# Rotation and scaling of queries and keys read by DVE straight from PSUM, in two transformer blocks on one core

## The chip, the cores and the metric

The kernel runs on one core of a Trainium2 chip, as one program in one launch. The core has TensorE (PE, matmuls into PSUM), VectorE (DVE), ScalarE (ACT), GpSimd (POOL) and a DMA queue issued from SyncE (SP). The metric is the device time in microseconds, the median of 3 runs of the whole program; the time before is 1341.64 us (1341.46 to 1342.78).

## The reference

Two transformer blocks over 512 positions and 1024 channels, float32. What touches the change is how each makes its queries and keys:

```
# block 1: 12 heads of 64, one dilated attention with three configurations
h = rms_norm(x, ln_pre_mix);  proj = h @ w_in
q, k = rope(q, pos), rope(k, pos)          # x1*cos - x2*sin, x2*cos + x1*sin
# block 2: 16 heads of 64 (differential, forgetting, chunked)
hn = rms_norm_2(h, ln_mix);  z = hn @ w_in
q1 = rms_norm_2(split_heads(q1, 4), g[0])  # the same for q2, k1, k2, qf, kf, qc, kc
```

After them come softmax, weighing of the values, an output projection, and a gated MLP (block 1) or a gated MLP with a short convolution and a last gate (block 2).

## The kernel before

Activations lie transposed, channels on the 128 partitions and the 512 positions along a row, in 8 tiles. Every float32 matrix product is done as three matmuls: each operand is split into a rounded high part and a rest (`wunit` for weights, lines 164 and 167; `split` for activations, lines 176 to 182), and high x high, high x low and low x high are added in PSUM (lines 186 to 188, and 372 to 374 for the projections).

PSUM has 8 banks, in four pools: 3 banks "d" for all that `psum()` asks for, 2 "s" for scores, 2 "t" for transposed probabilities and 1 "v" (`BANKS`, line 31). Tile frees a bank when the last instruction that reads it is done. Small work tiles of 128 x 512 come from rings, of which "z" has 6 slots.

A mixing stage is played from a list (`ORDER1`, `ORDER2`): P is a projection, T its transposes and head operands, V values, S scores, W weighing, U the pooled branch's input, O an early part of the output projection, D the first two projections of block 2 side by side, F the forget gate's rows, G the gate product of the end. Block 1 begins "P0 P2 P1 T0 V0 S00", block 2 "G0 G1 D VM P3 T1 T0 S00". Program order is a priority only: the order on each engine is made when the kernel is built, by a list schedule over a simulated timeline, and each engine then works through its own list in that order.

A projection (`chunk`, line 357) yields 256 columns, queries and keys of two heads. It runs in two halves of 2 x 128 positions; a half fills one bank of pool "d" with 48 matmuls, and then calls `out_of`. The normalisation is folded in afterwards: projections are made of the unnormalised activations, and the row statistic, a sum of squares over all 8 activation tiles, enters later as a factor per position.

In block 1, P0 is done with its contraction outermost, so that it can follow the arrival of the input, and both its halves end together. `rstd_cols` (lines 246 to 253) makes the statistic `rc` from the sum of squares by small matmuls (L249), Ln and Exp on ACT (L112) and three DVE steps (L234 to L236). Line 470 scales cosines and sines by it into `rot`. `out_of` (lines 482 to 495) copies the bank to z on ACT (L485); POOL makes the two products with the sine (L490, L491) into y; DVE multiplies by the cosine (L492) and adds the halves (L493, L494). `to_heads` (line 310) transposes z on TensorE (L316) into two banks of pool "d", from which ACT and DVE make high and low parts (L328 to L331), and DMAs copy rows across partitions (L418).

In block 2, `out_of` (lines 698 to 716) copies the bank to z (L700), squares it on ACT (L701), sums over each head on DVE (L703), multiplies by `r2`, made of `rc` (L665 to L667, L706), and gets the inverse root by Ln, Exp and three DVE steps (L710, L711, L713; L712 multiplies by `r1`, also made of `rc`). POOL then multiplies z by the result (L715). D uses `chunks_beside` (line 382): two projections share the contraction loop, and two banks are filled at a time. For these, `rc` comes from the second `rstd_cols` call, at the end of `post`, over the output of block 1.

Of the kernel before, what the change touches and what calls it, by code (L numbers as in the profile page):

```python
# [11 lines left out]
AF = mybir.ActivationFunctionType  # L12
ALU = mybir.AluOpType
AX = mybir.AxisListType

P = 128
# [45 lines left out]
class Builder:  # L62
# [386 lines left out]
    def mix1(self):  # L449
        nc = self.nc  # L450
        io = self.io
        x, h = [], []
        early = self.units("w_qk1", 0)
        for k in range(KD):
            x.extend(self.load_x((k,)))
            h.append(self.split(x[k], self.col("ln_pre_mix", k), tag="h"))
            if k in (0, 4):
                early(k // 4)
        self.rest()
        rope = self.slot("m", F32, (P, 4, 96))  # L460
        nc.sync.dma_start(rope, io["rope"])
        nc.sync.dma_start(self.ident, io["ident"])
        acc = self.slot("m")
        for k in range(KD):
            self.square_acc(acc, x[k], k == 0, after=self.last)
        R = self.slot("m")
        rc = self.rstd_cols(acc)
        rot = self.slot("m", F32, (P, 4, 96))
        for t in range(4):
            nc.vector.tensor_scalar(rot[:, t], rope[:, t], rc[:, 2 * t:2 * t + 1], None, ALU.mult)  # L470
        tab = self.slot("m")
        nc.sync.dma_start(tab, io["tab_mult"])

        zs = {}
        ops = {}
        ps = {}
        outs = {}

        def project(i):
            zs[i] = []  # L480

            def out_of(t1, ps):
                t0 = t1 - 1
                z, y = self.slot("z"), self.slot("z")
                nc.scalar.activation(z, ps, AF.Copy)  # L485
                zv, yv = [a.rearrange("p (t h d) -> p t h d", t=2, d=64) for a in (z, y)]
                cs = rot[:, t0:t0 + 2, 0:64].unsqueeze(2).to_broadcast([P, 2, 4, 64])
                sn = rot[:, t0:t0 + 2, 64:96].unsqueeze(2).to_broadcast([P, 2, 4, 32])
                a, b = slice(0, 32), slice(32, 64)
                nc.gpsimd.tensor_tensor(yv[:, :, :, a], zv[:, :, :, b], sn, ALU.mult)  # L490
                nc.gpsimd.tensor_tensor(yv[:, :, :, b], zv[:, :, :, a], sn, ALU.mult)  # L491
                nc.vector.tensor_tensor(zv, zv, cs, ALU.mult)  # L492
                nc.vector.tensor_tensor(zv[:, :, :, a], zv[:, :, :, a], yv[:, :, :, a], ALU.subtract)  # L493
                nc.vector.tensor_tensor(zv[:, :, :, b], zv[:, :, :, b], yv[:, :, :, b], ALU.add)  # L494
                zs[i].append(z)
            self.chunk("w_qk1", int(i), h, 256, out_of, i == "0", early)

        def heads(i):
            ops[i] = self.to_heads(zs[i], -0.125, None)

        oT = [None] * 8
        vts = []

        def values(g):
            vt = self.v_tiles()
            vts.append(vt)
            self.chunk("w_v1", int(g), h, 256, lambda t, ps: self.put_v2(vt, t, ps, rc))

        def score(i, e, wide=False):
            ps[i + e] = self.scores(ops[i][int(e)], tab, wide)  # L510

        def weigh(i, e, wide=False):
            i, e, p = int(i), int(e), ps[i + e]
            if e == 0:
                outs[i] = self.slot("o")
            j = (2 * i + e) % 4
            self.weigh(p, [vts[i // 2][t][:, j, :] for t in range(4)], outs[i], e == 1, wide)
            if e == 1:
                oT[2 + i] = self.split(outs[i], tag="o")

        us = []
        get = self.units("w_u1")

        def pool_in(i):
            if i == "0":
                self.rstd_rows(acc, R)
            u = self.psum()
            self.slab(u, "w_u1", int(i), h, units=get)
            t = self.slot("z")
            nc.vector.tensor_tensor(t, u, R, ALU.mult)  # L530
            us.append(t)

        self.play(ORDER1, P=project, T=heads, V=values, S=score, W=weigh, U=pool_in,
                  B=lambda: self.pool_branch(us, oT))
        return self.post(oT, DONE1, "w_out", "ln_post_mix", "ln_pre_ffn", True)
# [120 lines left out]
    def mix2(self, h, rc):  # L656
        nc = self.nc
# [31 lines left out]
        ps = {}  # L689
# [5 lines left out]
        def projected(i):  # L695
            out = zs[i] = []

            def out_of(t1, ps):
                z, sq = self.slot("z"), self.slot("z")
                nc.scalar.activation(z, ps, AF.Copy)  # L700
                nc.scalar.activation(sq, ps, AF.Square)  # L701
                st = self.small(8)
                nc.vector.tensor_reduce(st, sq.rearrange("p (h d) -> p h d", d=64), AX.X, ALU.add)  # L703
                four = lambda v: v[:, t1 - 1:t1 + 1].unsqueeze(2).to_broadcast([P, 2, 4])
                two = lambda v: v.rearrange("p (t h) -> p t h", h=4)
                nc.vector.tensor_tensor(two(st), two(st), four(r2), ALU.mult)  # L706
                y, w = self.small(8), self.small(8)
                self.act(y, st, AF.Ln, bias=self.eps, scale=1.0)
                self.act(y, y, AF.Exp, scale=-0.5)
                nc.vector.scalar_tensor_tensor(w, st, EPS, y, ALU.add, ALU.mult)  # L710
                nc.vector.scalar_tensor_tensor(w, w, -0.5, y, ALU.mult, ALU.mult)  # L711
                nc.vector.tensor_tensor(two(y), two(y), four(r1), ALU.mult)  # L712
                nc.vector.scalar_tensor_tensor(st, w, 1.5, y, ALU.add, ALU.mult)  # L713
                zv = z.rearrange("p (h d) -> p h d", d=64)
                nc.gpsimd.tensor_tensor(zv, zv, st.unsqueeze(2).to_broadcast([P, 8, 64]), ALU.mult)  # L715
                out.append(z)
            return out_of

# [100 lines left out]
        for m in range(KD):  # L819
            t = self.slot("v")  # L820
# [254 lines left out]
```

## Time and profile before

| | |
|---|---|
| median of 3 runs | 1341.64 us |
| the profiled execution's own time | 1343.58 us |
| its span, first to last instruction | 1341.5 us |
| PE busy | 1311.8 us (98%) |
| DVE busy | 851.3 us (63%) |
| ACT busy | 672.6 us (50%) |
| POOL busy | 153.8 us (11%) |
| mean granted TensorE clock | 0.994 |

The profile is one execution. Times of instructions count from the span's start. "L485" is line 485 of the kernel; a helper's line stands for all its callers, so L112 is every Ln, Exp and other special function. A row of waits or of the timeline says in brackets or after an arrow how long the engine had stood idle and which instruction ended that. [...]

Block 1's mixing takes about the first 200 us, its output projection and MLP run to about 615 us, block 2's mixing from there to about 890 us, and block 2's MLP and end the rest.

### The profile page before, as it was taken

Reading aid. Unit: us, or ns where it says so; the run is one execution under the profiler, and the core shown is the slowest. Engines: PE = TensorE matmul, PEld = TensorE weight load, DVE = VectorE, ACT = ScalarE, POOL = GpSimd, SP = SyncE. Lnnn points to the kernel's source line nnn. Section 1 sums busy time; section 2 is a strip of 40 time slices with the busy share of each in tenths; the row PEclk is TensorE's granted clock in tenths of the full one; section 3 lists DMA queues with packets and bytes.
Section 4 is the critical chain, followed back from the end, with each engine's and each line's share of the span. In section 5 each row is a group of like instructions: output and inputs, shape, how many; then the busy total and the mean of one; then the engine's idle time right before and its main releaser. Section 6 shows DMA issues by size and latency. Waiting matters only on the chain.

```text
span 1341.5 us, 20064 instructions
## 1 busy us (share of the span) xinstructions
PE 1311.8 (98%) x7450; PEld 1138.0 (85%) x7450; DVE 851.3 (63%) x1771; ACT 672.6 (50%) x1327; POOL 153.8 (11%) x190
## 2 busy tenths in 40 slices
PE   9799999999999999999999999899999999999998
PEld 9799988988888888888988999779888888888887
DVE  7777885864444432229588878766877777733354
ACT  6466755543333332237576777755554444522241
POOL 1232220000000000001222334430000000000000
PEclk9999999999999999999999999999999999999999
DMA  6322334233333333228244445333332332332221
GB/s 228 109 67 68 95 111 126 70 117 96 96 95 95 94 95 94 95 70 262 88 112 117 123 117 138 93 106 124 126 95 95 94 95 94 102 95 94 94 79 63
DMA packets 48801, 141.69 MB, mean 106 GB/s; under 512 B 6240, under 2 KB 7136, under 8 KB 48704
## 3 DMA queue, kind: packets, MB, share of 16 engines
q1 hardware_dynamic: 48704, 140.42, 34.0%
q8 instruction: 58, 0.95, 0.3%
q14 instruction: 39, 0.32, 0.1%
HBM read 122.38 MB, written 6.29 MB: 96 GB/s over the span
## 4 chain that ended last, share of the span: by engine, by line
PE 84%; DVE 8%; DMA 3%; ACT 2%; issue 2%; SPq 1%; POOL 0%; DVEq 0%; ACTq 0%; POOLq 0%
PE p L186 21%; PE p L187 21%; PE p L188 21%; PE p L372 4%; PE p L373 4%; PE p L374 4%; DVE wl L167 2%; PE p L283 2%; PE p L292 1%; PE p L291 1%; PE p L261 1%; DVE sp L265 1%; PE p L262 1%; DMA wr<-in_w_qk 1%; ACT sp L112 1%
## 5 line engine op out<-in xcount | busy, mean ns | idle before, releaser
L164 ACT ACTIVATE wh<-wr 128x512 fp32r<-128x512 f32 x417 | 259.2, 630 | 405.4 <-PE p L187 351.9
L167 DVE TENSOR_TENSOR wl<-wr,wh 128x512 fp32r<-128x512 f32 (+1 forms) x400 | 286.2, 723 | 238.5 <-ACT wh L164 227.1
L188 PE MATMUL p<-sh,wl 128*128 128x512 f32 (+1 forms) x858 | 320.4, 377 | 0.0
L187 PE MATMUL p<-sh,wh 128*128 128x512 f32 (+1 forms) x858 | 319.5, 376 | 0.1
L186 PE MATMUL p<-sh,wh 128*128 128x512 f32 (+1 forms) x858 | 311.0, 375 | 1.0 <-ACT sh L179 0.7
L372 PE MATMUL p<-wh,sh 128*128 128x256 f32 (+1 forms) x672 | 193.3, 289 | 5.8 <-ACT sz L485 3.3
L373 PE MATMUL p<-wl,sh 128*128 128x256 f32 (+1 forms) x672 | 192.1, 287 | 0.3 <-DVE wl L167 0.2
L374 PE MATMUL p<-wh,sh 128*128 128x256 f32 (+1 forms) x672 | 191.2, 286 | 0.0
L187 PEld LDWEIGHTS p<-sh,wh 128*128 128x128 f32 x858 | 161.2, 188 | 32.6 <-issue 0.5
L188 PEld LDWEIGHTS p<-sh,wl 128*128 128x128 f32 x858 | 161.2, 188 | 31.8 <-issue 0.7
L186 PEld LDWEIGHTS p<-sh,wh 128*128 128x128 f32 x858 | 157.2, 188 | 33.4 <-ACT sh L179 1.1
L372 PEld LDWEIGHTS p<-wh,sh 128*128 128x128 f32 x672 | 128.7, 192 | 9.1 <-ACT sz L485 3.6
L373 PEld LDWEIGHTS p<-wl,sh 128*128 128x128 f32 x672 | 128.9, 192 | 1.1 <-DVE wl L167 0.8
L374 PEld LDWEIGHTS p<-wh,sh 128*128 128x128 f32 x672 | 128.6, 192 | 1.1 <-issue 0.5
L273 POOL TENSOR_SCALAR sp<-sp,m 128x128 f32<-128x128 f32 (+1 forms) x112 | 72.0, 647 | 186.3 <-DVE m L269 145.5
L112 ACT ACTIVATE sp<-sp,m 128x128 f32<-128x128 f32 (+3 forms) x128 | 71.5, 560 | 36.4 <-DVE m L265 33.8
L188 PE MATMUL p<-so,wl 128*128 128x512 f32 (+1 forms) x246 | 88.5, 360 | 0.0
L187 PE MATMUL p<-so,wh 128*128 128x512 f32 (+1 forms) x246 | 88.5, 360 | 0.0
L186 PE MATMUL p<-so,wh 128*128 128x512 f32 (+1 forms) x246 | 87.6, 361 | 0.6 <-DVE m L265 0.5
L167 POOL TENSOR_TENSOR wl<-wr,wh 128x512 fp32r<-128x512 f32 (+1 forms) x17 | 23.8, 1402 | 455.3 <-ACT wh L164 443.7
L265 DVE CUSTOM_DVE_ANT_0 sp<-p,sm 128x128 f32<-128x128 f32 (+3 forms) x128 | 60.4, 483 | 17.3 <-PE p L262 13.5
L187 PE MATMUL p<-sk,wh 128*128 128x512 f32 (+1 forms) x184 | 67.1, 365 | 0.0
(205 smaller groups left out, 2138.8 us busy)
## 6 DMA issues: line engine op xcount, KB each, us to landing
wr<-in_w_gu SPq DMA_DIRECT2D x88, 512.0 KB
wr<-in_w_down SPq DMA_DIRECT2D x44, 512.0 KB
wr<-in_w_qk SPq DMA_DIRECT2D x31, 512.0 KB
sk<-sk SPq DMA_DIRECT2D x88, 128.0 KB
wr<-in_w_out SPq DMA_DIRECT2D x12, 512.0 KB
sv<-in_x SPq DMA_DIRECT2D x16, 256.0 KB
wr<-in_w_ple_gate SPq DMA_DIRECT2D x8, 512.0 KB
wr<-in_w_v SPq DMA_DIRECT2D x6, 512.0 KB
```

The lines of the kernel that those rows point to most:

```text
L112: i = self.nc.scalar.activation(out, in_, func, **k)
L164: nc.scalar.activation(hi[:, :w], c, AF.Copy)
L167: eng.tensor_tensor(lo[:, :w], c, hi[:, :w].bitcast(F32), ALU.subtract)
L186: mm(out, lhsT=ahi, rhs=bhi, start=start, stop=False)
L187: mm(out, lhsT=ahi, rhs=blo, start=False, stop=False)
L188: mm(out, lhsT=alo, rhs=bhi, start=False, stop=stop)
L265: nc.vector.tensor_tensor_reduce(p[:, :n], ps[:, :n], tab[:, (3 - qb) * P:S], 1.0, 3e38, ALU.add, ALU.min, accum_out=m[:, 0:1])
L273: self.nc.gpsimd.tensor_scalar(p[:, :n], p[:, :n], m[:, 2:3], 1.0, ALU.mult, ALU.mult)
L283: ins = nc.tensor.transpose(pt[:, w:w + P], ps_list[qb][:, kb * P:kb * P + P], self.ident)
L372: mm(d, lhsT=h[k][0][:, a], rhs=hi[:, c], start=k == 0 and (o == 0 or not first), stop=False)
L373: mm(d, lhsT=h[k][0][:, a], rhs=lo[:, c], start=False, stop=False)
L374: mm(d, lhsT=h[k][1][:, a], rhs=hi[:, c], start=False, stop=k == 7 and (o > 0 or not first))
```

## The change

In block 1 ACT's copy of the bank is gone. DVE makes the product with the cosine and both products with the sine straight from PSUM, and the two last steps are as before. In block 2 the copy is gone too, and the product with the inverse root is made by DVE from PSUM into z in place of POOL's from z to z. The square still reads the bank on ACT. Nothing else is edited.

```
--- before.py
+++ after.py
@@ -482,14 +482,13 @@
             def out_of(t1, ps):
                 t0 = t1 - 1
                 z, y = self.slot("z"), self.slot("z")
-                nc.scalar.activation(z, ps, AF.Copy)
-                zv, yv = [a.rearrange("p (t h d) -> p t h d", t=2, d=64) for a in (z, y)]
+                zv, yv, pv = [a.rearrange("p (t h d) -> p t h d", t=2, d=64) for a in (z, y, ps)]
                 cs = rot[:, t0:t0 + 2, 0:64].unsqueeze(2).to_broadcast([P, 2, 4, 64])
                 sn = rot[:, t0:t0 + 2, 64:96].unsqueeze(2).to_broadcast([P, 2, 4, 32])
                 a, b = slice(0, 32), slice(32, 64)
-                nc.gpsimd.tensor_tensor(yv[:, :, :, a], zv[:, :, :, b], sn, ALU.mult)
-                nc.gpsimd.tensor_tensor(yv[:, :, :, b], zv[:, :, :, a], sn, ALU.mult)
-                nc.vector.tensor_tensor(zv, zv, cs, ALU.mult)
+                nc.vector.tensor_tensor(zv, pv, cs, ALU.mult)
+                nc.vector.tensor_tensor(yv[:, :, :, a], pv[:, :, :, b], sn, ALU.mult)
+                nc.vector.tensor_tensor(yv[:, :, :, b], pv[:, :, :, a], sn, ALU.mult)
                 nc.vector.tensor_tensor(zv[:, :, :, a], zv[:, :, :, a], yv[:, :, :, a], ALU.subtract)
                 nc.vector.tensor_tensor(zv[:, :, :, b], zv[:, :, :, b], yv[:, :, :, b], ALU.add)
                 zs[i].append(z)
@@ -697,7 +696,6 @@
 
             def out_of(t1, ps):
                 z, sq = self.slot("z"), self.slot("z")
-                nc.scalar.activation(z, ps, AF.Copy)
                 nc.scalar.activation(sq, ps, AF.Square)
                 st = self.small(8)
                 nc.vector.tensor_reduce(st, sq.rearrange("p (h d) -> p h d", d=64), AX.X, ALU.add)
@@ -711,8 +709,8 @@
                 nc.vector.scalar_tensor_tensor(w, w, -0.5, y, ALU.mult, ALU.mult)
                 nc.vector.tensor_tensor(two(y), two(y), four(r1), ALU.mult)
                 nc.vector.scalar_tensor_tensor(st, w, 1.5, y, ALU.add, ALU.mult)
-                zv = z.rearrange("p (h d) -> p h d", d=64)
-                nc.gpsimd.tensor_tensor(zv, zv, st.unsqueeze(2).to_broadcast([P, 8, 64]), ALU.mult)
+                zv, pv = [a.rearrange("p (h d) -> p h d", d=64) for a in (z, ps)]
+                nc.vector.tensor_tensor(zv, pv, st.unsqueeze(2).to_broadcast([P, 8, 64]), ALU.mult)
                 out.append(z)
             return out_of
 
```

## Rows read from the trace of the kernel before

**Rows 1.** The page: busy time of each engine; the chain that ended last.
```profile
PE 1311.8 (98%) x7450; PEld 1138.0 (85%) x7450; DVE 851.3 (63%) x1771; ACT 672.6 (50%) x1327; POOL 153.8 (11%) x190
PE 84%; DVE 8%; DMA 3%; ACT 2%; issue 2%; SPq 1%; POOL 0%; DVEq 0%; ACTq 0%; POOLq 0%
```
**Rows 2.** TensorE's waits: waiter, releaser: total us, times, longest us.
```profile
PE p L372 <- ACT sz L485: 3.3, 1, 3.3
...
PE p L261 <- DMA sk<-sk: 2.3, 1, 2.3
```
**Rows 3.** Timeline, start of block 1: start us, duration us, engine, line.
```profile
17.99 0.57 ACT L485 ACTIVATE sz<-p 128x512 f32<-128x512 f32 x1
...
24.05 0.95 PE L249 MATMUL p<-ones,sm 128*128 128x2 f32 x8
...
27.59 0.97 DVE L470 TENSOR_SCALAR sm<-sm,rc 128x96 f32<-128x96 f32 x4
...
41.54 1.03 PE L316 MATMUL p<-ident,sz 128*128 128x128 f32 x8
```
**Rows 4.** Windows: stretch and length, busy us per engine, granted clock, DMA.
```profile
45.90:51.60 5.70, 5.68 (x48) 5.68 (x48) 5.61 (x9) 2.63 (x5) 2.16 (x2) 1.00 0.56 176
...
54.20:58.20 4.00, 4.00 (x21) 4.00 (x22) 0.14 (x1) 0.00 (x0) 0.00 (x0) 0.57 0.08 18
...
640.00:860.00 220.00, 210.83 (x1637) 200.29 (x1636) 175.90 (x520) 155.25 (x374) 75.08 (x88) 0.99 0.40 113
```
**Rows 5.** Groups by line: count, then busy us, mean ns, idle before.
```profile
L167 DVE TENSOR_TENSOR wl<-wr,wh 128x512 fp32r<-128x512 f32 (+1 forms) x400 | 286.2, 723 | 238.5 <-ACT wh L164 227.1 <-PE p L187 5.2 <-PE p L188 3.5
...
L898 DVE TENSOR_TENSOR sz<-p,sm 128x512 f32<-128x512 f32 x44 | 30.3, 688 | 27.1 <-PE p L188 27.0
...
L715 POOL TENSOR_TENSOR sz<-sz,m 128x512 f32<-128x512 f32 x20 | 22.5, 1124 | 41.9 <-DVE m L713 34.5 <-ACT st L295 4.4 <-DVE m L269 2.9
...
L908 DVE TENSOR_TENSOR sz<-sz,sz 128x512 f32<-128x512 f32 x22 | 15.1, 686 | 0.0
...
L700 ACT ACTIVATE sz<-p 128x512 f32<-128x512 f32 x20 | 11.9, 593 | 5.6 <-PE p L374 4.3 <-PE p L397 1.1
...
L490 POOL TENSOR_TENSOR sz<-sz,sm 128x256 f32<-128x256 f32 x12 | 11.3, 945 | 47.9 <-DVE sm L470 27.3 <-ACT sz L485 15.7 <-DVE sz L494 4.9
...
L492 DVE TENSOR_TENSOR sz<-sz,sm 128x512 f32<-128x512 f32 x12 | 8.7, 729 | 5.1 <-POOL sz L491 5.1
...
L485 ACT ACTIVATE sz<-p 128x512 f32<-128x512 f32 x12 | 7.0, 592 | 8.9 <-DVE sz L494 7.1 <-PE p L374 1.7
...
L493 DVE TENSOR_TENSOR sz<-sz,sz 128x256 f32<-128x256 f32 x12 | 5.7, 472 | 0.1
```
**Rows 6.** Timelines of ACT, PE and DVE at the start of block 2.
```profile
635.46 0.58 ACT L701 ACTIVATE sz<-p 128x512 f32<-128x512 f32 x1
...
637.93 0.41 PE L395 MATMUL p<-wh,sh 128*128 128x256 f32 x1
...
641.82 0.50 PE L249 MATMUL p<-ones,sz 128*128 128x2 f32 x4
...
643.64 0.17 DVE L236 SCALAR_TENSOR_TENSOR rc<-m,rc 128x8 f32<-128x8 f32 x1
...
648.72 0.17 DVE L713 SCALAR_TENSOR_TENSOR m<-m,m 128x8 f32<-128x8 f32 x1
```
**Rows 7.** Timelines of ACT, DVE and PE, 663 to 682 us.
```profile
663.24 0.60 ACT L700 ACTIVATE sz<-p 128x512 f32<-128x512 f32 x1 [1.82 <-PE p L374]
...
665.08 0.17 DVE L706 TENSOR_TENSOR m<-m,r 128x8 f32<-128x8 f32 x1
...
666.46 0.17 DVE L713 SCALAR_TENSOR_TENSOR m<-m,m 128x8 f32<-128x8 f32 x1
...
673.97 0.63 PE L316 MATMUL p<-ident,sz 128*128 128x128 f32 x4 [1.40 <-DVE sk L329]
...
681.34 0.34 PE L261 MATMUL p<-sk,sk 128*128 128x128 f32 x2
```

More of the change, by code (lines that the diff above doesn't have):

```diff
@@ L484, in out_of @@
                 z, y = self.slot("z"), self.slot("z")
-                nc.scalar.activation(z, ps, AF.Copy)
-                zv, yv = [a.rearrange("p (t h d) -> p t h d", t=2, d=64) for a in (z, y)]
+                zv, yv, pv = [a.rearrange("p (t h d) -> p t h d", t=2, d=64) for a in (z, y, ps)]
                 cs = rot[:, t0:t0 + 2, 0:64].unsqueeze(2).to_broadcast([P, 2, 4, 64])
@@ L489, in out_of @@
                 a, b = slice(0, 32), slice(32, 64)
-                nc.gpsimd.tensor_tensor(yv[:, :, :, a], zv[:, :, :, b], sn, ALU.mult)
-                nc.gpsimd.tensor_tensor(yv[:, :, :, b], zv[:, :, :, a], sn, ALU.mult)
-                nc.vector.tensor_tensor(zv, zv, cs, ALU.mult)
+                nc.vector.tensor_tensor(zv, pv, cs, ALU.mult)
+                nc.vector.tensor_tensor(yv[:, :, :, a], pv[:, :, :, b], sn, ALU.mult)
+                nc.vector.tensor_tensor(yv[:, :, :, b], pv[:, :, :, a], sn, ALU.mult)
                 nc.vector.tensor_tensor(zv[:, :, :, a], zv[:, :, :, a], yv[:, :, :, a], ALU.subtract)
@@ L699, in out_of @@
                 z, sq = self.slot("z"), self.slot("z")
-                nc.scalar.activation(z, ps, AF.Copy)
                 nc.scalar.activation(sq, ps, AF.Square)
@@ L713, in out_of @@
                 nc.vector.scalar_tensor_tensor(st, w, 1.5, y, ALU.add, ALU.mult)
-                zv = z.rearrange("p (h d) -> p h d", d=64)
-                nc.gpsimd.tensor_tensor(zv, zv, st.unsqueeze(2).to_broadcast([P, 8, 64]), ALU.mult)
+                zv, pv = [a.rearrange("p (h d) -> p h d", d=64) for a in (z, ps)]
+                nc.vector.tensor_tensor(zv, pv, st.unsqueeze(2).to_broadcast([P, 8, 64]), ALU.mult)
                 out.append(z)
```

## The prediction, made before the result was known

> **What bounds the kernel now.** I read the busy shares and chain first. TensorE is busy 98% of the span and 84% of the chain that ended last is matmul [rows 1], so an edit on DVE, ACT or POOL moves the time only where a matmul waits for it. The page of the profile doesn't say where. The second view is TensorE's waits: the longest is 3.3 us of a projection or value matmul for ACT's copy L485, an instruction that the change deletes, then 2.3 us for a DMA of head rows [rows 2]. Both lie at the start of block 1. The third view is the timeline of both starts [rows 3, 6], because there TensorE has only one kind of work ready: projections, values and transposes, all of which take a bank of the three-bank pool "d". The other five banks belong to scores, transposes of probabilities and weighing, which can't begin before the first heads are made. The reader should see in rows 3 and 6 when a bank is given back, and when its next user wants it.
>
> **What the change does to a bank.** Before, a projection's bank is free once ACT has copied it (block 1: 0.59 us; block 2: copy and square, 0.59 us each) [rows 5]. Neither copy needs the row statistic. After, block 1's bank is held until DVE has read it three times, and all three reads need the cosines and sines already scaled by the statistic (L470); block 2's bank is held until the whole chain square, reduce, Ln, Exp, four small DVE steps is through and DVE has multiplied. So at each start the bank's release moves from "the matmuls are done" to "the row statistic is done".
>
> **Work removed and added.** Block 1 has 12 tiles (6 projections, 2 halves). Gone: 12 copies of 0.59 us on ACT = 7.1, and 24 POOL products of 0.94 us (the 12 of L490 and the same 12 of L491) = 22.6. Added on DVE: 24 products on 256 columns; the trace has no such product from PSUM, so I take L493's 0.47 us (the same columns, from SBUF): 11.3. The product with the cosines stays, now from PSUM, and costs the same. Block 2 has 20 tiles. Gone: 20 x 0.59 = 11.9 on ACT and 20 x 1.12 = 22.5 on POOL. Added on DVE: 20 products on 512 columns from PSUM, nearest row L898, 0.69 us: 13.8 [rows 5]. ACT and POOL bound nothing here, so what they lose is worth nothing unless a wait for them ended last.
>
> [...]
>
> **Start of block 1: +1.0 us.** One half of a projection takes 5.7 us (48 matmuls in 5.68) [rows 4]. T0's transposes start at 41.54 right behind three halves (P2's second, P1's two) and the 0.95 us of L249, so P2's second half began at 41.54 - 3 x 5.68 - 0.95 = 23.55. It takes the bank of P0's first half, which ACT had copied at 17.99 to 18.56 [rows 3]. After the change that bank waits for L470, which ends at 28.56, and then for three DVE reads, 0.73 + 2 x 0.47 = 1.67: 30.2. TensorE has nothing else except L249 itself, so the loss is 30.2 - 23.55 - 0.95 = 5.7. If the statistic ran without waits (in block 2 it takes 1.5 us from the end of L249 to L236's end [rows 6], and L470 0.97, against 3.6 here) and L249 followed at 23.55, the loss would be 1.1 + 0.5 less: 4.1. [...]
>
> Much of this is paid back soon. The 3.3 us wait for L485 came from ACT's copy standing behind POOL and DVE; after, the first value half waits only for P1's second half to be rotated, 1.67 us, of which the transposes hide 1.03: 2.7 back. The 2.3 us wait for head rows [rows 2] shrinks too, as ACT reaches the heads sooner; I take 2.0. [...] Sum 5.7 + 1.7 - 2.7 - 2.0 - 1.7 = +1.0; ends -2.6 (4.1 - 2.7 - 2.3 - 1.7) and +7.4 (nothing paid back).
>
> **Start of block 2: +7 us.** Step D runs the first two projections together and fills two banks, then two more. Its fourth tile takes the bank of its first. Before, the square of the first tile ended at 636.04, and the fourth tile began at 637.93 [rows 6], without waiting. After, that bank waits for rc, and rc needs L249, which ran at 641.82, in the middle of the fourth tile; rc was done at 643.81 (end of L236), and the tile's scale at 648.89 (end of L713) [rows 6]. Worst case, all that keeps its time: 648.89 + 0.69 = 649.6, so 11.7 late, less 0.5 for L249 that no longer lies inside the tile: +11.2. Best case, L249 goes at 637.93 when TensorE runs dry, rc follows 2.0 us later as it did (639.9), r1 and r2 take 0.6 (three steps of L236's size with their gaps), L706 to the end of L713 1.55 as under light load [rows 7], the product 0.69: 642.8, +4.4. ACT and DVE keep their weight splits, placed by a schedule made at build, among these steps, as before, so I take 7, a little below the middle. No scores are ready to fill this hole.
>
> **T0 of block 2: +1.5 us.** P3's second half used to give its bank back after 1.2 us; now after 3.4 (L700 at 663.24 to the end of L713 at 666.63) - 0.6 + 0.7 = 3.5 at best. T0 follows T1 at once and already waited 1.40 us for T1's bank [rows 7]; it loses its alternative. Ends 0 and +3.
>
> **The rest of block 2: +1.5 us.** From 640 to 860 us DVE is busy 175.9 of 220, and TensorE idle 9.2 [rows 4]. With 13.8 more, DVE goes from 80% to 86%, so what waits for DVE waits longer; scores and weighing fill most holes. Ends -2 (POOL's hop out of the chain) and +9 (TensorE's idle time doubles). Block 1's later tiles are counted at nothing: they hold a bank 1.67 us instead of 0.59, behind halves of 5.7. If that cover fails, they cost up to 1.1 each for 6 tiles, inside the ends above.
>
> **Sum.** 1.0 + 7 + 1.5 + 1.5 = +11.0. The profiled execution took 1343.58 us (span 1341.5), 1.94 over the median of 1341.64; the same step on the median gives 1352.6.
>
> **Rivals.** (a) Banks starve all through block 2: the other 16 tiles (20 less D's 4) each delay the next user by 1 us more, on top: 1341.6 + 11 + 16 = about 1368. For it: every P is followed by transposes that want two banks. Against: only 2.3 us of longer hold beside halves of 5.7, and scores to fill in with from 681 us on [rows 7]. (b) It is hidden: block 1 pays back all and the schedule made at build brings the statistic early in block 2, so the ends -2.6, +4.4, 0 and -2 meet: 1341.4, no change. (c) Faster: the hop ACT, POOL, DVE was the real drag. Its place is the start of block 1, its price 3.3 + 2.3 + 1.7 = 7.3, so 1334.3 if the new schedule gives P0's and D's first banks back before they are wanted. It decides once both starts together lose under 7.3 gross. For it: L485 tops the waits. Against: L470 and rc come from sums that the change doesn't speed up, and D alone loses 4.4 at best. DVE also gets some time back: its weight splits average 0.723 us where a quiet product takes 0.686 [rows 5], 400 x 0.037 = 14.8 us, and POOL loses 45.1 of its 153.8 us [rows 1, 5], so perhaps 4 us of DVE. [...]
>
> **How the numbers follow.** Forecast 0.66, (a) 0.08, (b) 0.12, (c) 0.12, and 0.02 for a reshuffled order that I can't price. The forecast's own range is 1345 to 1364. The range of 8 in 10 runs from (b)'s near side to just short of (a): 1341 to 1366. A difference of 0.2%, 2.7 us, is about what can be told from no change: faster 0.12, within 0.10, slower 0.78.
>
> **What would show it.** In the new trace, TensorE idle for 4 to 6 us between 23 and 31 us, ended by DVE's read of the first projection; another 4 to 10 us hole before the fourth tile of step D, ended by the product that replaces L715; no wait for L485. L485, L490, L491 and L700 gone, DVE 25 us busier, POOL 45 us less. If either hole is missing, or D's hole is paid back before 700 us, the prediction is wrong; if the loss lies after 700, rival (a) is right.

## The result, and the profile after

The changed kernel takes 1377.22 us (median of 4 runs, 1374.89 to 1377.86) against 1342.21 us for the kernel before on the same chip: a ratio of 1.0261 [1.024, 1.0283], about 35 us slower. The prediction had 1352.6 us, with a range to 1366: the direction was right, the size too small by 25 us.

In the kernel after, lines from 493 to 699 have a number one lower than before, and lines from 701 one that is two lower: L489 is the product with the cosine, L490 and L491 are those with the sine, L699 is the square, L708 to L711 the last small steps, L713 the product with the inverse root. The page gives the busy time of each engine and the chain that ended last [rows 1]:

```profile
PE 1325.8 (96%) x7450; PEld 1146.1 (83%) x7450; DVE 861.8 (63%) x1815; ACT 658.5 (48%) x1295; POOL 107.2 (8%) x146
...
PE 84%; DVE 10%; ACT 3%; issue 2%; DMA 2%; SPq 0%; POOL 0%; DVEq 0%; ACTq 0%; POOLq 0%
```

The span grew from 1341.5 to 1375.8 us. TensorE does the same 7450 matmuls, but is busy 14.0 us longer (the mean granted clock, a share of TensorE's full speed, fell from 0.994 to 0.985), and stands idle 50.0 us in place of 29.7. So 20.3 of the 34.3 us are idle time; of the 14.0 us of longer work some 8 are the price of the lower clock (an estimate, worked out with rows 4 below), and the rest is not explained. TensorE's waits after (waiter, releaser: us in total, times, longest) name several causes, and none is large [rows 2]:

```profile
PE p L261 <- DVE m L265: 6.1, 13, 0.9
PE p L372 <- DVE sz L491: 5.7, 2, 4.5
PE p L395 <- DVE sz L713: 4.7, 1, 4.7
PE p L261 <- DMA sk<-sk: 4.1, 2, 2.9
PE p L283 <- DVE st L177: 3.4, 2, 2.5
```

Two of these are the holes that the prediction looked for. The first, at the start of block 1 (timeline of PE and DVE: start, duration, engine, line) [rows 3]:

```profile
25.40 0.95 PE L249 MATMUL p<-ones,sm 128*128 128x2 f32 x8
...
29.41 0.83 DVE L470 TENSOR_SCALAR sm<-sm,rc 128x96 f32<-128x96 f32 x4
...
30.15 0.69 DVE L489 TENSOR_TENSOR sz<-p,sm 128x512 f32<-128x512 f32 x1
30.75 0.42 DVE L490 TENSOR_TENSOR sz<-p,sm 128x256 f32<-128x256 f32 x1
31.08 0.42 DVE L491 TENSOR_TENSOR sz<-p,sm 128x256 f32<-128x256 f32 x1
...
31.64 0.55 PE L372 MATMUL p<-wh,sh 128*128 128x256 f32 x1 [4.48 <-DVE sz L491]
...
51.15 1.03 PE L316 MATMUL p<-ident,sz 128*128 128x128 f32 x8
...
53.45 0.36 PE L372 MATMUL p<-wh,sh 128*128 128x256 f32 x1 [1.26 <-DVE sz L491]
```

P2's second half starts at 31.64, when the third DVE read has freed the bank, instead of at 23.55 as the prediction had worked out for the kernel before. T0's transposes start 9.6 us late (51.15 against 41.54). Some 1.4 us of this are there already at 14 us, before any bank is held (the first squares for the statistic, L224, begin at 14.20 instead of 12.78); block 2's edit alone, which leaves block 1 as it was, has them too (T0's transposes at 43.0). The second hole, at the start of block 2 [rows 6], and the start of T0 [rows 7]:

```profile
642.71 0.61 PE L249 MATMUL p<-ones,sz 128*128 128x2 f32 x4 [0.21 <-DVE sz L228]
...
644.80 0.17 DVE L236 SCALAR_TENSOR_TENSOR rc<-m,rc 128x8 f32<-128x8 f32 x1
...
647.18 0.69 DVE L713 TENSOR_TENSOR sz<-p,m 128x512 f32<-128x512 f32 x1
...
648.02 0.55 PE L395 MATMUL p<-wh,sh 128*128 128x256 f32 x1 [4.70 <-DVE sz L713]
...
683.83 0.41 PE L316 MATMUL p<-ident,sz 128*128 128x128 f32 x2 [1.96 <-DVE sz L713]
```

Where the 34.3 us were lost is read from the same landmarks in both traces (lines of the kernel before):

| landmark | before | after | late |
|---|---|---|---|
| T0's transposes, block 1 (L316) | 41.5 | 51.2 | +9.6 |
| input of the pooled branch, U0, is read (L530) | 170.5 | 173.7 | +3.2 |
| last gated tile of block 1's end (L582) | 607.2 | 612.6 | +5.4 |
| T1 of block 2 begins (L316) | 668.7 | 678.3 | +9.6 |
| N0, norm of a weighed head pair (L785) | 749.0 | 772.8 | +23.8 |
| N1 (L785) | 784.0 | 810.1 | +26.1 |
| fifth of the nine adds of block 2's mixing output (L876) | 917.0 | 951.3 | +34.3 |
| last read of the end (L941) | 1336.5 | 1370.8 | +34.3 |

Block 1 lost 5.4 us, step D 4.2, and the rest of block 2's mixing 24.7. That last stretch, by windows (start:end, length, then busy us of PE, PEld, DVE, ACT and POOL with counts, granted clock, and the DMA engines' share and GB/s), in the kernel before and then after [rows 4]:

```profile
668.70:917.00 248.30, 238.16 (x1680) 216.94 (x1679) 193.49 (x539) 172.09 (x410) 81.32 (x99) 0.99 0.39 110
```

```profile
678.30:951.30 273.00, 251.27 (x1680) 225.36 (x1680) 199.01 (x554) 167.20 (x395) 62.23 (x84) 0.96 0.36 100
...
702.50:706.10 3.60, 1.61 (x7) 0.89 (x6) 3.54 (x12) 3.58 (x11) 0.00 (x0) 1.00 0.58 154
706.10:712.50 6.40, 5.92 (x24) 5.28 (x25) 6.21 (x30) 3.71 (x12) 1.83 (x4) 0.50 0.42 118
```

For the same 1680 matmuls TensorE is idle 21.7 us instead of 10.1 and busy 13.1 us longer. The two short windows show how the two go together: after 3.6 us in which it worked 1.6, the granted clock falls to 0.50, the lower of the two levels in the trace's clock records (1.00 and 0.50), and TensorE is busy for 5.92 of the next 6.4 us at that level. By these records it spent 23.9 us of this stretch at the lower level, 21.3 of them at work, and 3.4 in the kernel before. There, matmuls of 256 columns start 0.21 us apart instead of 0.12. By this the lower clock cost some 9 us instead of 1.5 (an estimate), so about 8 of the 13.1; what made the rest longer is not shown.

### The profile page after: what moved, and what is told of

The parts are those of the page before. It is cut to its first block, busy times and chain, and to the rows that moved or that the text cites. A ratio compares the mean times of both kernels' runs of the same rounds, so it can differ in the third digit from the quotient of the medians.

```text
span 1375.8 us, 20029 instructions
## 1 busy us (share of the span) xinstructions
PE 1325.8 (96%) x7450; PEld 1146.1 (83%) x7450; DVE 861.8 (63%) x1815; ACT 658.5 (48%) x1295; POOL 107.2 (8%) x146
## 4 chain that ended last, share of the span: by engine, by line
PE 84%; DVE 10%; ACT 3%; issue 2%; DMA 2%; SPq 0%; POOL 0%; DVEq 0%; ACTq 0%; POOLq 0%
PE p L186 21%; PE p L187 21%; PE p L188 21%; PE p L372 5%; PE p L373 5%; PE p L374 5%; DVE wl L167 2%; PE p L283 1%; DVE sp L265 1%; PE p L292 1%; PE p L291 1%; PE p L261 1%; DMA wr<-in_w_qk 1%; PE p L262 1%; DVE sh L180 1%
## 5 line engine op out<-in xcount | busy, mean ns | idle before, releaser
L167 DVE TENSOR_TENSOR wl<-wr,wh 128x512 fp32r<-128x512 f32 (+1 forms) x400 | 279.0, 704 | 240.4 <-ACT wh L164 229.5
L372 PE MATMUL p<-wh,sh 128*128 128x256 f32 (+1 forms) x672 | 197.3, 294 | 8.3 <-DVE sz L491 5.7
L373 PE MATMUL p<-wl,sh 128*128 128x256 f32 (+1 forms) x672 | 195.8, 292 | 0.6 <-DVE wl L167 0.5
L374 PE MATMUL p<-wh,sh 128*128 128x256 f32 (+1 forms) x672 | 194.3, 291 | 0.0
L372 PEld LDWEIGHTS p<-wh,sh 128*128 128x128 f32 x672 | 132.9, 198 | 11.0 <-issue 5.8
L373 PEld LDWEIGHTS p<-wl,sh 128*128 128x128 f32 x672 | 132.9, 198 | 2.0 <-DVE wl L167 1.5
L374 PEld LDWEIGHTS p<-wh,sh 128*128 128x128 f32 x672 | 132.0, 197 | 0.9 <-DVE sh L180 0.3
L112 ACT ACTIVATE sp<-sp,m 128x128 f32<-128x128 f32 (+3 forms) x128 | 71.5, 559 | 40.4 <-DVE m L265 37.5
L273 POOL TENSOR_SCALAR sp<-sp,m 128x128 f32<-128x128 f32 (+1 forms) x112 | 68.0, 613 | 282.3 <-DVE m L269 236.5
L265 DVE CUSTOM_DVE_ANT_0 sp<-p,sm 128x128 f32<-128x128 f32 (+3 forms) x128 | 60.1, 482 | 16.4 <-PE p L262 14.8
L188 PE MATMUL p<-sk,wl 128*128 128x512 f32 (+1 forms) x184 | 67.0, 364 | 0.0
```

The lines of the kernel that those rows point to most:

```text
L112: i = self.nc.scalar.activation(out, in_, func, **k)
L167: eng.tensor_tensor(lo[:, :w], c, hi[:, :w].bitcast(F32), ALU.subtract)
L188: mm(out, lhsT=alo, rhs=bhi, start=False, stop=stop)
L265: nc.vector.tensor_tensor_reduce(p[:, :n], ps[:, :n], tab[:, (3 - qb) * P:S], 1.0, 3e38, ALU.add, ALU.min, accum_out=m[:, 0:1])
L273: self.nc.gpsimd.tensor_scalar(p[:, :n], p[:, :n], m[:, 2:3], 1.0, ALU.mult, ALU.mult)
L372: mm(d, lhsT=h[k][0][:, a], rhs=hi[:, c], start=k == 0 and (o == 0 or not first), stop=False)
```

## The experiments

The theory to be tested (theory 1, the bank, in the expectations) is that the change costs by holding a bank of pool "d" longer, until the row and head statistics are done. Its first rival (theory 2) is that DVE's added load delays what TensorE waits for. Later the theory was split: by 1a TensorE really waits for the late banks; by 1b the list schedule made at build, which sees the late banks in its simulated timeline, lays down a worse order, and that order costs time by itself. All ratios are against runs of the kernel before beside them. Nothing of the computation is left out in any of these kernels.

**Each block's edit alone.** The change's diff, cut to its first hunk (block 1):

```
-                nc.scalar.activation(z, ps, AF.Copy)
...
+                nc.vector.tensor_tensor(zv, pv, cs, ALU.mult)
+                nc.vector.tensor_tensor(yv[:, :, :, a], pv[:, :, :, b], sn, ALU.mult)
+                nc.vector.tensor_tensor(yv[:, :, :, b], pv[:, :, :, a], sn, ALU.mult)
```

> Only block 1's edit (DVE rotates from PSUM; block 2 as before). The landmarks of the two traces split the 35 us as +5.5 up to block 1's output projection, +4.2 at step D and +24.7 behind it. If the parts add up, this kernel is 5 to 6 us slower than before (about 1347.5), with the hole of some 5 us behind P2's first half. If the slow part of block 2 came out of a reshuffle that block 1's edit starts, block 2 would be longer here too, and the kernel 10 us or more slower.

and to its other two (block 2):

```
-                nc.scalar.activation(z, ps, AF.Copy)
...
+                nc.vector.tensor_tensor(zv, pv, st.unsqueeze(2).to_broadcast([P, 8, 64]), ALU.mult)
```

> Only block 2's edit (no copy, DVE scales from PSUM; block 1 as before). If the parts add up: 28 to 30 us slower than before (about 1371). If the two edits meet in one schedule made at build and only together make it bad, clearly less, 10 to 20 us.

Measured: block 1 alone 1345.36 us, 1.0027 [1.0014, 1.0041], so +3.6 (5 to 6 was expected); block 2 alone 1373.02 us, 1.0232 [1.0213, 1.0251], so +31. The two add up to the whole change (0.27% + 2.32% against 2.61%). Block 2 is what has to be explained.

**Load or hold.** The first kernel puts the load on DVE but keeps ACT's copy, so the bank is free early; the second keeps POOL's product, but makes ACT's copy only after the chain, by a scale of 1 that depends on its result, so that the bank is held and DVE gains one small step.

```
-                nc.gpsimd.tensor_tensor(zv, zv, st.unsqueeze(2).to_broadcast([P, 8, 64]), ALU.mult)
+                nc.vector.tensor_tensor(zv, zv, st.unsqueeze(2).to_broadcast([P, 8, 64]), ALU.mult)
```

> Block 2: ACT's copy is kept, so the bank is free after copy and square, but the product is made by DVE (from z in SBUF) in place of POOL. It has DVE's extra 13.8 us without the long hold of the bank. Theory 1, the bank: within 4 us of before (1338 to 1346). Theory 2, DVE's load: most of block 2's loss, 20 us or more (1362 and up). Theory 3, any edit here reshuffles the schedule made at build: a few us either way, 5 to 10.

```
-                nc.scalar.activation(z, ps, AF.Copy)
...
+                ob = self.small(1)
+                nc.vector.tensor_scalar(ob, st[:, 0:1], 0.0, 1.0, ALU.mult, ALU.add)
+                nc.scalar.activation(z, ps, AF.Copy, scale=ob)
```

> Block 2: ACT's copy is kept but made after the chain (its scale operand is a 1.0 computed from the chain's result, one DVE step of one column per tile more), and POOL still makes the product. The bank is held about as long as after the change, without DVE's 13.8 us. Theory 1, the bank: 20 to 30 us slower than before (1362 to 1372). Theory 2, DVE's load: under 8 us slower (below 1350), the hole at step D alone.

Measured: the load alone 1344.46 us, 1.0015 [1.0, 1.0029], some 2 us; the hold alone 1383.91 us, 1.0314 [1.0295, 1.0333], some 42 us, with DVE at 853.5 us, almost as before. The load falls as the cause. The late copy is enough for the loss; that it costs more than the 20 to 30 us expected may come from T's input, which is later here too, behind the copy and POOL's product, and this share was not separated from the hold. TensorE's waits in the two kernels (L715 is DVE's product in the first and the late copy in the second):

```profile
PE p L372 <- ACT sz L485: 3.2, 1, 3.2
...
PE p L261 <- DVE m L265: 1.4, 4, 0.7
```

```profile
PE p L261 <- DVE m L265: 8.7, 12, 2.1
PE p L395 <- ACT sz L715: 5.3, 1, 5.3
```

The hold shows as one wait of 5.3 us for the held bank itself, and beyond it as longer waits of scores (L261) for a softmax step of DVE.

**Is it the three banks?** Block 2's edit, with T's transposes taken out of pool "d" and put into the two banks of "t"; beside it the kernel before with the same move, as a control.

```
-        qT, kT = self.psum(), self.psum()
+        qT, kT = (self.psum(), self.psum()) if gk is None else (self.psT(), self.psT())
```

> Block 2's edit alone (it measured +31 us), but block 2's head transposes take their two banks from the two-bank pool of the transposed probabilities, not from the projections' pool. Theory 1a, the projections' pool is short of banks: most of the loss behind step D comes back, 12 to 20 us, so 1353 to 1361; step D's hole stays, for no transposes lie in it. Theory 1b, the loss is the order that the schedule made at build gives TensorE, whatever the pool: no better than 1366.

> The same move of block 2's head transposes in the kernel before, as the control: the projections' pool isn't short there, so within 4 us of before, or a few us slower where transposes now wait for weighing's banks.

Measured: with block 2's edit 1351.32 us, 1.0085 [1.006, 1.0111]; in the control 1346.31 us, 1.0037 [1.002, 1.0055]. The move costs some 5 us in the kernel before, and yet gives back some 20 of the 31 us with the change (1.0085 against 1.0232). Against the control, block 2's edit costs 5.0 us more, about what D's hole alone takes: its wait stands unchanged at 4.9 in the waits of this kernel (L714 is the product):

```profile
PE p L283 <- DVE sk L329: 5.5, 2, 3.3
PE p L395 <- DVE sz L714: 4.9, 1, 4.9
```

So the longer hold costs because projections, values and T's transposes take turns on three banks.

**The first tiles alone.** Step D keeps copy and POOL product in block 2, the other 16 tiles are as changed; and P0 keeps them in block 1, the other 10 tiles are as changed.

```
+                early = int(i) < 2
+                if early:
+                    nc.scalar.activation(z, ps, AF.Copy)
...
+                if early:
+                    nc.gpsimd.tensor_tensor(zv, zv, st.unsqueeze(2).to_broadcast([P, 8, 64]), ALU.mult)
+                else:
+                    nc.vector.tensor_tensor(zv, pv, st.unsqueeze(2).to_broadcast([P, 8, 64]), ALU.mult)
```

> Block 2's edit, but step D's two projections keep ACT's copy and POOL's product: four of the twenty tiles give their bank back early. It prices the hole at step D. The landmarks say 4 to 5 us: so 26 us slower than before remain (1366 to 1370). If the order of all that follows hangs on that hole, 10 us or more come back (under 1363).

> Block 1's edit alone (it measured +3.6 us), but projection 0, whose bank waits for the row statistic, keeps ACT's copy and POOL's products; block 2 as before. If the loss in block 1 is that hole: the same as before or up to 3 us faster (1338 to 1343). If it is DVE's 11 us of products: still 3 us slower.

Measured: with D copied 1365.03 us, 1.0177 [1.015, 1.0204]. Each against the kernel before beside it, that is about 7 us less than block 2's edit whole (1.0232), so D's four tiles cost about 7 of the 31, and the loss behind D stays. With P0 copied 1338.43 us, 0.9983 [0.997, 0.9996]: block 1's edit turns from +3.6 to -2.3 us. P0's two tiles were its whole loss. The 3.3 us wait for L485 [rows 2] becomes this one, for the last sine product of a later projection:

```profile
PE p L372 <- DVE sz L498: 2.8, 1, 2.8
```

**Held bank or order made at build.** Behind D, TensorE's 1903 instructions of block 2 were tied into a fixed order by dependencies that add no semaphore: block 2's edit in the order of the kernel before, and the kernel before in the order that block 2's edit had got. Tied to its own order, the kernel before builds into the very same instructions, so the tie adds nothing by itself. The lists of DVE and ACT are made at build around the tied one.

```
+        h = self.ffn1(*self.mix1())
+        n = len(self.pe)
+        out = self.mix2(*h)
+        part = self.pe[n + 240:n + 2143]
+        order = pe_order()
...
+        for a, b in zip(order, order[1:]):
+            self.after(part[b], part[a].name)
```

> Block 2's edit alone (it measured +31 us), but TensorE's instructions of block 2's mixing and output projection behind step D (1903 of them) are held to the very order that they have in the kernel before; the other engines' orders are made at build around it. Theory 1b, the loss is the order that the build's schedule gives TensorE because it expects the banks late: most of the 25 us behind D comes back, so 1346 to 1354, with step D's 5 us left. Theory 1a, TensorE really waits for the banks: no gain, the waits now stand before the projections and transposes, 1365 to 1375.

> The counterpart: the kernel before, with every copy and every early release, but the same 1903 instructions of TensorE are held to the order that they have in the kernel with block 2's edit. Theory 1b: 15 to 25 us slower than before though no bank is held long (1356 to 1367). Theory 1a: within 5 us of before.

Measured: block 2's edit in the old order 1379.16 us, 1.0266 [1.0251, 1.0282], some 36 us slower; the kernel before in the new order 1373.78 us, 1.0232 [1.0215, 1.0249], some 31. The first run goes the way that 1a forecast, the second the way of 1b, and both lose more than was forecast: neither form alone covers both. TensorE's waits of the first, and one start of a half in its timeline (TensorE's line is L120 throughout, L375 is L329 of the kernel before, L746 the square, L760 the product):

```profile
PE p L120 <- DVE sk L375: 18.0, 4, 6.0
PE p L120 <- DVE sz L760: 4.9, 1, 4.9
```

```profile
697.70 1.04 PE L120 MATMUL p<-ident,sz 128*128 128x128 f32 x8
...
698.00 0.57 ACT L746 ACTIVATE sz<-p 128x512 f32<-128x512 f32 x1
...
705.16 0.55 PE L120 MATMUL p<-wh,sh 128*128 128x256 f32 x1 [5.16 <-DVE sk L375]
...
707.22 0.69 DVE L760 TENSOR_TENSOR sz<-p,m 128x512 f32<-128x512 f32 x1
```

In the old order three starts of a projection or value wait 16.0 us in all until DVE has read T's banks (the other 2.0 us are a start of T itself). The rows show why: T fills two banks at 697.70, the half squared at 698.00 keeps the third until its product at 707.22, and so the next half must wait for T's readers. In the second kernel no projection or value waits for T's banks, and its waits (L119 is TensorE, L310 is L265 of before) are those of the changed kernel's own order:

```profile
PE p L119 <- DVE m L310: 9.5, 11, 2.0
PE p L119 <- DMA sk<-sk: 6.5, 2, 3.6
PE p L119 <- DVE st L222: 5.3, 6, 3.0
```

Scores and weighing stand and wait for softmax steps, splits and head rows, at a granted clock of 0.984: in an order made for late banks the loss is there without the late banks. I read the two runs together so: the shortage of banks is paid either in waits for the bank (old order) or in an order that steps round them (the build's own), and neither order escapes it; the build's own is the cheaper by some 0.3% (1.0232 against 1.0266, intervals that just touch).

**D mended, in the old order.** D copied as above, and the order of the kernel before behind it.

> Block 2's edit with step D's four tiles copied as before, and TensorE behind D in the old order: sixteen tiles are still held through their chain and multiplied by DVE from PSUM. Theory 1b: within 4 us of before (1338 to 1346). Theory 1a: 15 us or more slower.

Measured: 1368.94 us, 1.02 [1.0185, 1.0215]. By 1b it should have been near the kernel before; it is 27 us slower, with the same 18.0 us of waits for L375. The 16 tiles behind D hold their banks too long for the old order too.

**All three cures.** The change with P0 and D copied and T's transposes in "t".

> The whole change with all three places closed at once: projection 0 of block 1 and step D's two projections of block 2 keep ACT's copy and POOL's products, and block 2's head transposes take the other pool. DVE still makes 20 of its 24 new sine products and 16 of its 20 new scalings from PSUM. If the three places are the whole cause: the control with the moved transposes (+5 us) less block 1's 2 us, so 1341 to 1348. If the long hold or DVE's load costs anywhere else: 1352 or more.

Measured: 1343.88 us, 1.0024 [1.0012, 1.0036]. The 35 us are all but gone, at a clock of 0.993, with 26 of the 32 tiles still read from PSUM by DVE (all but P0's two and D's four). It is no gain over the kernel before; the move of T by itself costs some 5 us there. The one version below both kernels is block 1's edit with P0 copied, by 2.3 us.

## Why the prediction was wrong

**What was right.** Both holes are where the prediction put them, and are ended by the named reads: 4.48 us ending at 31.64 (forecast 4 to 6) and 4.70 us before D's fourth tile (4 to 10). The wait for L485 is gone. D's cost of +7: the landmarks give 4.2, D copied saves about 7. T0 of block 2 waits 1.96 us instead of 1.40 (forecast +1.5, with an end at 0). POOL lost 46.6 us (forecast 45).

**The step that failed: the rest of block 2, +1.5 us; it was +24.7.** Its sum looked at how full DVE would be and found room; DVE's load is worth 2 us. The hold had been sized in the step before, at T0, as 1.2 us before and 3.5 after, from the one chain of rows 7, which ran nearly undisturbed, and rival (a) was turned down with "only 2.3 us of longer hold". Rows 7 is the least of 20 chains. Over the 20 tiles of the kernel before, the way from L700's start to L713's end takes 3.4 to 15.8 us, 8.6 in the mean; here is another one of its timeline:

```profile
699.42 0.60 ACT L700 ACTIVATE sz<-p 128x512 f32<-128x512 f32 x1
...
706.25 0.17 DVE L713 SCALAR_TENSOR_TENSOR m<-m,m 128x8 f32<-128x8 f32 x1
```

It takes 7.0 us for what takes 3.4 in rows 7, and such a row could have been read before the change. After the change, one like it holds a bank:

```profile
723.29 0.60 ACT L699 ACTIVATE sz<-p 128x512 f32<-128x512 f32 x1
...
727.43 0.21 ACT L112 ACTIVATE m<-m 128x8 f32<-128x8 f32 x1
...
727.70 0.67 DVE L177 TENSOR_TENSOR st<-p,st 128x512 fp32r<-128x512 f32 x1
728.41 0.76 DVE L329 SCALAR_TENSOR_TENSOR sk<-p,gq,sk 64x512 fp32r<-64x512 f32 x1
729.20 0.17 DVE L708 SCALAR_TENSOR_TENSOR m<-m,m 128x8 f32<-128x8 f32 x1
...
731.24 0.69 DVE L713 TENSOR_TENSOR sz<-p,m 128x512 f32<-128x512 f32 x1
```

8.6 us, because the small steps stand in the engines' lists behind large ones: Exp (L112) is done at 727.64, but the step that uses it (L708) comes at 729.20, behind L177 and L329. The mean hold of the 20 tiles went from 1.43 us (copy and square) to 7.05 (square to product): 5.6 us more, not 2.3, and longer than a half of 5.7 us [rows 4]. Eight of the 20 are over 8 us. Rival (a) had the right cause, banks short all through block 2, and the prediction's own sign for it ("if the loss lies after 700") is what the landmarks show: 24.7 us behind T1. Its price of 1 us for each of 16 tiles was low for the same reason, and it left the clock out, which makes up about a third of the loss (some 8 of 24.7). Its picture, the next user kept waiting at the bank, is what the old order shows; in the changed kernel the shortage came as another order, the "reshuffled order" that the prediction gave 0.02 and no price, and that costs 31 us even with every bank free early.

**"Scores to fill in with".** This clause against (a) failed too. Scores did fill in, but each takes one of the two banks of pool "s" and can follow only when DVE's softmax step (L265) has read it, so they wait in turn (13 times, 6.1 us in all, against 5 times and 2.5 before, all in block 2); and behind such a row of waits the clock fell to 0.50 at 706.1 us [rows 4].

**Start of block 1: +1.0, and it was +5.4 by 612 us** (+3.6 for block 1's edit alone). The hole was sized well, and what was to be paid back came almost in full: T0's transposes are 9.6 us late, the scores that start at 65.5 us (68.9 after) only 3.4, so 6.2 us came back of a forecast 6.4 (2.7 + 2.0 + 1.7). The 1.7 us for a low clock, which the sum adds once and takes off once and which is in rival (c)'s price too, is an estimate that no run shows as lost time. The clock records show 3.41 us at 0.50 from 54.50 us on in the kernel before, and none there in the changed one, which has 6.83 us at 0.50 from 30.27 us on. The first value half waits 1.26 us instead of 3.3, and the wait for head rows in block 1 is gone; the 4.1 us of such waits in the list [rows 2] lie in block 2. Of what is left over the forecast, 1.4 us stood before the hole, and some 2 us came near the end of the mixing, where the prediction had counted block 1's later tiles at nothing. The first row is of the kernel before, the others of the changed one:

```profile
54.15 0.47 PE L261 MATMUL p<-sk,sk 128*128 128x128 f32 x2 [2.30 <-DMA sk<-sk]
```

```profile
167.57 0.47 PE L186 MATMUL p<-sh,wh 128*128 128x512 f32 x1 [2.00 <-DVE sv L414]
...
732.02 0.66 PE L261 MATMUL p<-sk,sk 128*128 128x128 f32 x2 [2.87 <-DMA sk<-sk]
```

The wait of 2.00 us was 0.24: DVE's new list has the value split L414 behind two softmax steps. It stands in both kernels with block 1's edit alone too (2.02 and 2.01), with P0 copied or not.

**DVE +25 us: it was +10.5.** The added products cost 10.0 + 13.7 = 23.7. Much came back, which the prediction had only as a guess of 4 us. Groups by line (count, busy us, mean ns, idle before) [rows 5]:

```profile
L167 DVE TENSOR_TENSOR wl<-wr,wh 128x512 fp32r<-128x512 f32 (+1 forms) x400 | 279.0, 704 | 240.4 <-ACT wh L164 229.5 <-PE p L188 7.1 <-PE p L187 1.4
...
L713 DVE TENSOR_TENSOR sz<-p,m 128x512 f32<-128x512 f32 x20 | 13.7, 687 | 0.6
...
L489 DVE TENSOR_TENSOR sz<-p,sm 128x512 f32<-128x512 f32 x12 | 8.2, 685 | 2.5 <-PE p L374 2.4
...
L490 DVE TENSOR_TENSOR sz<-p,sm 128x256 f32<-128x256 f32 x12 | 5.0, 414 | 0.0
...
L492 DVE TENSOR_TENSOR sz<-sz,sz 128x256 f32<-128x256 f32 x12 | 5.0, 416 | 0.0
```

The 400 weight splits went from 723 to 704 ns, 7.2 us in all, and L493's step (now L492) from 472 to 416.

**What stays open.** That the hold on three banks is the cause is shown (late copy alone +42, load alone +2, T's transposes on other banks some -20). How its 31 us divide between direct waits and order is not: the old order has the first, the new order the second, and T's transposes on other banks take both away at once. A fourth bank for pool "d" was not tried.

## What to carry to other kernels

Before a copy out of PSUM is dropped, take the time from the bank's fill to its new last reader over all tiles of the loaded stretch, mean and longest, and hold it against the time in which the next user of the pool comes round; a chain of small steps through busy engines was here as long as their queues made it, not as its instructions (3.4 to 15.8 us for the same steps). Where the first tiles of a stage wait for a statistic, they can keep the copy while the others drop it (P0 copied turned +3.6 into -2.3 us). And when TensorE's waits don't add up to a loss, look at the clock and at the order of the work: here the wait on the bank was a small part of what the bank cost.

## What the runs showed of the hardware

A DVE product from PSUM was no dearer than one from SBUF: 414 against 416 ns on 256 columns, 685 and 687 against 686 on 512 [rows 5]. The weight splits (L167, both inputs in SBUF) got 19 ns shorter in the mean because fewer of them met POOL. In the kernel before, the 356 of 396 that no POOL instruction overlaps take 688 ns, the 40 others 1047; after, 376 take 687 and 20 take 1031. No split that runs alone takes over 696. That accounts for the 7.2 us. L493's mean of 472 ns goes the same way: ten of its 12 took 402 to 425 ns before, three of them beside POOL, and the other two 694 and 845, both beside POOL. POOL's products are slower there as well: L490 takes 0.73 us alone (at 117.01 us) and 0.74 beside L265, which reads PSUM (at 78.39), but 1.18 beside L167 and L492 (at 30.27). One case of L492 beside POOL and one without, in the kernel before:

```profile
30.27 1.18 POOL L490 TENSOR_TENSOR sz<-sz,sm 128x256 f32<-128x256 f32 x1
30.77 1.22 DVE L492 TENSOR_TENSOR sz<-sz,sm 128x512 f32<-128x512 f32 x1
...
36.02 0.68 DVE L492 TENSOR_TENSOR sz<-sz,sm 128x512 f32<-128x512 f32 x1
```

The mean shows it poorly: the kernel that keeps all of POOL's products and holds the bank has 719 ns, and each block's edit alone 720 and 716.

The granted clock fell to 0.50 at 706.1 us, behind 3.6 us with 1.61 us of work in which no single gap was over 0.9 us [rows 4]. A row of short gaps came before a low clock here, with no long one among them.
